# Gathering two expert jobs' tokens with one product, pairing attention units, and a sixth weight buffer

## The chip, the cores and the metric

The kernel runs on one core of a Trainium2 chip. The metric is the device time of one launch in microseconds (us). A core has a matrix engine (TensorE, PE in the rows), which loads a stationary operand ("weight load", PEld) and streams a moving one past it; a vector engine (DVE), a scalar engine (ACT), GpSimd (POOL), a sync engine (SP) that here only issues transfers, and 16 DMA engines. Matrix results land in PSUM, all other on-chip data in SBUF.

## The reference

Two networks run one behind the other on 256 tokens of 1024 features, in fp32.

```python
def first_block(...):                    # depth 2
    for i in range(2):
        u = rmsnorm(h, norm_mix[i])
        h = h + (dsw_mixer if i == 0 else moba_mixer)(u, ...)     # attention a, attention b
        h = h + sq_relu_mlp(rmsnorm(h, norm_ffn[i]), ffn_w1[i], ffn_w2[i])
# dsw_mixer: 3 groups of 8 heads, logits + rel_bias[bucket(dist * dilation)], band masks,
#            the groups' outputs weighted by softmax of their log-sums; moba_mixer: 16 heads

def second_block(x, c, ctx, ...):        # depth 2
    mod = silu(c) @ mod_w[i] + mod_b[i]  # shifts, scales, gates
    yx, yc = (_mixer_ab if i == 0 else _mixer_cd)(...)   # grouped attention, 8 heads, 2 key heads;
                                                         # with a convolution (AB) or a pooling (CD)
    x = x + g1 * yx                      # ctx, 256 tokens, too in layer 0
    out = _moe(tokens, ...)              # 512 tokens in layer 0, 256 in layer 1

def _moe(h, ...):                        # 32 experts, 2 for each token
    xb = h_pad[tok]                      # the tokens of one expert, gathered
    hid = silu(xb @ w_gate[e]) * (xb @ w_up[e])
    return (hid @ w_down[e]) * wt        # added back to the tokens' rows
```

## The kernel before

The stages follow one another, with parts of the next stage pulled into the one that runs (`defer` and `tick` put small steps between matmuls). In the profiled execution they stand about here: 0 to 152 us attention a's projection, to 230 its attention units and output, to 440 the first feed-forward part, to 548 attention b, to 840 the second feed-forward part with the context half of mixer AB, to 1085 the rest of AB and the routing, 1086 to 1616 the experts of layer 0 ("MoE0"), to 1775 mixer CD and the routing, 1778 to 2242 the experts of layer 1 ("MoE1").

**Weights.** All big weights come in units of 1 MB, in the order of one list, issued by SP (`pump`, L242). A unit goes into a ring of RING = 5 SBUF buffers, into smaller rings in some stages, or into SBUF that a stage leaves free; a unit is issued when `consumed` reports that an earlier one has been used.

**Bias table** (`bias_vectors`, L683 to L694). Relative-position biases for 40 heads are made early, in the first projection: four matmuls (one for each of the 3 groups of 8 heads, one for 16 heads) multiply the 33 x heads table `rb` with one-hot rows `oh`. Each result, 8 or 16 partitions of 384 numbers, is copied to `b`, and a POOL-issued DMA writes it 32 times to the DRAM buffer `bd` (the 32 copies let `Bias.fetch` read 128 shifted rows, L709).

**Attention units.** A unit is one head's or some heads' logits for 128 queries (`Attention`, `Unit`). `feed` issues the logits of one unit (L883 for attention a and b, L1155 for the grouped mixers) and its exponentials; `step` transposes a unit's probabilities (L780) and multiplies them with the values (L791). With `pair` 2 (all but attention a) the value products of two units are issued alternately. A head's 64 features lie in partitions 0 to 63 or 64 to 127, so a logits matmul uses half of the rows of TensorE; the heads of one unit all use the same half. Up to three units are fed ahead. PSUM has 6 buffers `acc` and 2 buffers `trp`.

**Modulation.** Between the units, `step` of the modulation multiplies 2 units `fw` of `mod_w` (L631); the next two are issued from there (L615).

**Experts** (L1910 to L2254). Two experts make a job of 128 slots, one expert in each half. 16 jobs; MoE0 has a 17th, "extra". For a job, DVE makes the one-hot matrix `P` (token x slot, `match`, L1924). The tokens are kept as two fp32r parts `hi` and `lo`, token rows on partitions. `gather` multiplies `P` as the stationary operand with the tokens (L1935 `hi`, L1936 `lo`; 128 x 512 each, 16 in MoE0 with four token tiles, 8 in MoE1 with two), giving slots on partitions; ACT copies that to `G`. `turn` transposes `G` in 8 blocks (L1949), and DVE copies to `XT`, features on partitions. `project` (L2000) multiplies `XT` with gate and up weights, `hidden_T` (L2023) transposes the product, `down` (L2038) multiplies with the down weights, `combine` (L2047) adds the result to the tokens. While job i runs, job i+1's gather and its transposes stand between `hidden_T` and `down`, and in the middle of `down`.

Behind job OVER = 7 in MoE1, and behind "extra" (index 8) in MoE0, stands a loop for experts with too many tokens (L2216 to L2232). It is skipped in the run shown, where nothing overflows. Before it the last job is combined; after it the next job is gathered from the start (`first_half`).

## Time and profile before

| | us |
|---|---|
| median of 3 runs | 2248.01 |
| lowest, highest | 2244.2, 2254.72 |
| the profiled execution's own time | 2244.44 |
| its span in the trace | 2242.3 |
| busy in the span: PE / DVE / ACT / POOL | 2055.0 / 1052.6 / 802.8 / 482.9 |

A row of the profile's timeline has the start in us, the length in us, the engine, the line, the operation, the tile written and those read, the shapes, and a count of like instructions in a row; in brackets stands how long the engine was idle before, and what released it. A matmul's end is modelled: neighbours overlap in the rows, and the distance of their starts is what one costs.

### The profile page before, as it was taken

What the parts mean: (1) busy time and instruction counts of PE and PEld (TensorE: products, weight loads), DVE (VectorE), ACT (ScalarE), POOL (GpSimd) and SP (SyncE); (2) the same over time, 40 slices, a digit from 0 to 9 for tenths busy, and PEclk for the clock granted to TensorE, in tenths of its full rate; (3) what the DMA queues carried; (4) which work ended last, traced back from release to release, by engine and by line L of the source; (5) the groups of instructions that cost most, each with busy time, mean ns of one, the idle gap of its engine ahead of it and who ended that gap; (6) DMA issues with size and microseconds to landing.
All of it is one profiled execution on the core that took longest, in us unless ns stands there. A gap on an engine that the chain in (4) does not pass through costs nothing. (4 is left out here: it accounts for less than half of the span.)

```text
span 2242.3 us, 28204 instructions
## 1 busy us (share of the span) xinstructions
PE 2055.0 (92%) x10811; PEld 1296.0 (58%) x10811; DVE 1052.6 (47%) x2077; ACT 802.8 (36%) x1454; POOL 482.9 (22%) x431
## 2 busy tenths in 40 slices
PE   7699999999998699689799997999889799989998
PEld 5476888776997588357444453444365544433443
DVE  6544645664758955966533332333463422222222
ACT  5344544555666566544211111111164411211111
POOL 1000010100116610403233232323330111211111
PEclk9899999999999999688899999999999899999999
DMA  9966677775654343104699996999742699999998
GB/s 259 269 240 239 207 252 264 232 264 176 204 180 151 123 140 112 36 32 162 268 409 406 403 405 269 406 405 402 298 148 80 243 418 421 420 420 384 421 420 346
DMA packets 160701, 612.97 MB, mean 273 GB/s; under 512 B 10599, under 2 KB 16135, under 8 KB 111280
## 3 DMA queue, kind: packets, MB, share of 16 engines
q1 hardware_dynamic: 155744, 596.86, 69.4%
q0 software_dynamic: 4384, 13.51, 3.0%
q8 instruction: 87, 1.43, 0.3%
q10 hardware_dynamic: 432, 0.74, 0.1%
q14 instruction: 54, 0.44, 0.1%
HBM read 607.90 MB, written 3.16 MB: 273 GB/s over the span
## 5 line engine op out<-in xcount | busy, mean ns | idle before, releaser
L2000 PE MATMUL acc<-w,XT 128*64 128x512 f32 x1856 | 430.6, 594 | 2.9 <-DMA w<-in_ex_up_dram 2.8
L301 DVE TENSOR_TENSOR w<-w 128x1024 fp32r<-128x1024 f32 x244 | 306.7, 1270 | 196.7 <-ACT w L300 192.2
L300 ACT ACTIVATE w<-w 128x1024 fp32r<-128x1024 f32 x252 | 264.4, 1057 | 187.8 <-PE acc L321 92.5
L2000 PEld LDWEIGHTS acc<-w,XT 128*64 128x64 f32 x1856 | 140.8, 137 | 252.6 <-issue 230.7
L2059 POOL TENSOR_TENSOR X<-X,tm 128x512 f32<-128x512 f32 x124 | 155.7, 1283 | 426.6 <-DVE tm L2057 426.6
L2057 DVE TENSOR_TENSOR tm<-acc,gate 128x512 f32<-128x512 f32 x196 | 129.7, 687 | 213.0 <-PE acc L2047 167.1
L2038 PE MATMUL acc<-w,hT 128*64 128x512 f32 x912 | 215.3, 598 | 1.5 <-ACT hT L2026 1.5
L363 PE MATMUL acc<-hi,w 128*128 128x256 f32 x576 | 165.6, 288 | 8.0 <-ACT qn L1094 3.8
L364 PE MATMUL acc<-lo,w 128*128 128x256 f32 x576 | 163.1, 283 | 0.8 <-POOL lo L490 0.8
L365 PE MATMUL acc<-hi,w 128*128 128x256 f32 x576 | 162.9, 283 | 0.7 <-DVE w L301 0.7
L321 PE MATMUL acc<-w,lo 128*128 128x512 f32 x368 | 150.3, 408 | 1.7 <-POOL lo L1368 1.6
L319 PE MATMUL acc<-w,hi 128*128 128x512 f32 x336 | 143.5, 427 | 7.7 <-ACT hi L1367 6.3
L320 PE MATMUL acc<-w,hi 128*128 128x512 f32 x336 | 137.6, 410 | 9.0 <-DVE w L301 8.8
L2059 POOL TENSOR_TENSOR C<-C,tm 128x512 f32<-128x512 f32 x64 | 79.6, 1275 | 286.5 <-DVE tm L2057 286.5
L2026 ACT ACTIVATE hT<-trp 128x512 f32<-128x512 f32 (+1 forms) x33 | 19.6, 593 | 325.7 <-PE trp L2023 325.7
L2017 DVE SCALAR_TENSOR_TENSOR hd<-sg,ws,acc 128x512 f32<-128x512 f32 (+1 forms) x33 | 36.2, 1098 | 187.6 <-issue 95.8
L2038 PEld LDWEIGHTS acc<-w,hT 128*64 128x64 f32 x912 | 62.4, 136 | 101.4 <-issue 99.1
L363 PEld LDWEIGHTS acc<-hi,w 128*128 128x128 f32 x576 | 110.5, 192 | 11.2 <-ACT qn L1094 4.0
L1304 POOL TENSOR_TENSOR cy<-cy,tap 128x256 f32<-128x256 f32 x90 | 88.8, 1007 | 119.4 <-ACT tap L1303 68.3
L365 PEld LDWEIGHTS acc<-hi,w 128*128 128x128 f32 x576 | 111.4, 193 | 0.9 <-DVE w L301 0.9
L320 PE MATMUL acc<-w,hh 128*128 128x512 f32 x256 | 102.2, 399 | 10.6 <-DVE w L301 10.4
L417 ACT ACTIVATE Yh<-acc 128x512 fp32r<-128x512 f32 x63 | 37.6, 598 | 206.5 <-PE acc L2038 202.8
(431 smaller groups left out, 3671.8 us busy)
## 6 DMA issues: line engine op xcount, KB each, us to landing
w<-in_ex_gate_dram SPq DMA_DIRECT2D x118, 1024.0 KB, 11.3
w<-in_ex_up_dram SPq DMA_DIRECT2D x118, 1024.0 KB, 12.5
w<-in_ex_down_dram SPq DMA_DIRECT2D x118, 1024.0 KB, 9.5
w<-in_ffn_w_dram SPq DMA_DIRECT2D x64, 1024.0 KB, 5.3
fw<-in_mod_w_dram SPq DMA_DIRECT2D x48, 1024.0 KB, 7.4
w<-in_a_w_qkv_dram SPq DMA_DIRECT2D x17, 1024.0 KB, 13.0
w<-in_w_in_ab_dram SPq DMA_DIRECT2D x14, 1024.0 KB, 5.2
w<-in_b_w_qkv_dram SPq DMA_DIRECT2D x12, 1024.0 KB, 5.3
```

The lines of the kernel that those rows point to most:

```text
L300: nc.scalar.activation(wh, w, AF.Copy)
L301: self.engine.tensor_tensor(wl, w, wh.bitcast(F32), op=OP.subtract)
L319: nc.tensor.matmul(ps[:, :n], xh, wh, start=first, stop=False)
L320: nc.tensor.matmul(ps[:, :n], xh, wl, start=False, stop=False)
L321: nc.tensor.matmul(ps[:, :n], xl, wh, start=False, stop=last)
L363: nc.tensor.matmul(z, wh[:, js], xh, start=k == 0 and j % 2 == 0, stop=False)
L364: nc.tensor.matmul(z, wh[:, js], xl, start=False, stop=False)
L365: nc.tensor.matmul(z, wl[:, js], xh, start=False, stop=k == 7 and j % 2 == 1)
L2000: nc.tensor.matmul(p[self.rows(a)], self.XT[:, 4 * k0 + k, self.rows(a)], units[v + a][:, k], start=k0 + k == 0, stop=4 * k0 + k == 7)
L2038: nc.tensor.matmul(self.p[c][self.rows(a)], self.hT[:, 2 * n + k, self.rows(a)], units[v + a][:, k, s], start=n + k == 0, stop=n + k == 2)
L2057: nc.vector.tensor_tensor(g, p, gates[s][:, c], op=OP.mult)
L2059: add.tensor_tensor(dst, dst, g, op=OP.add)
```

## The change

- `bias_vectors`: the table is widened on DVE so that each head's column stands 32 times (`wide`); ten matmuls of 4 heads each give all 128 partitions at once; DVE and ACT copy the results in turn; 16 DMAs write `bd` from 64 or 128 partitions without repeating a source row. The order of `bd`'s heads changes with it.
- `Attention`: two units are always fed together, their logits matmuls issued alternately, and one unit uses the upper and the other the lower half of the rows. Attention a gets paired value products too. Up to four units are fed ahead.
- Experts: `Group` gathers for two jobs at once: the tokens are the stationary operand (128 x 128 blocks) and `P` of 256 slots moves, so that the result has features on partitions and needs no transposes: 64 matmuls of 128 x 256 for two jobs in MoE0, 32 in MoE1. Every second job has no gather. The copies to `XT` alternate between ACT and DVE. MoE0's 17th job is gathered alone, at 256 columns.
- The loop stands behind job index 8 in both layers, and the job behind it is gathered before it.
- RING is 6; some small tiles are shared by both layers, and a scratch size for POOL's DMA descriptors is given.

```diff
-RING = 5
+RING = 6
...
+            wide = wk.tile([33, 24, 32], F32, name="wide")
+            nc.vector.tensor_copy(wide, b_(rb[:, :, None], [33, 24, 32]))
+
+            for i, h0 in enumerate([*range(0, 24, 4), *range(0, 16, 4)]):
+                g = min(i // 2, 3)
+                p = acc()[:, 0:384]
+                nc.tensor.matmul(p, wide[:, h0:h0 + 4].rearrange("r h c -> r (h c)"), oh[:, g], start=True, stop=True)
+                b = wk.tile([128, 384], F32, name="b", bufs=10)
+                if i % 2:
+                    nc.scalar.activation(b, p, AF.Copy)
+                else:
+                    nc.vector.tensor_copy(b, p)
+
+                for a, r, n in [(2 * a, 3 * (h0 % 8) + 6 * a + 2 * g, 2) for a in range(2)] if g < 3 else [(0, 24 + h0, 4)]:
+                    nc.gpsimd.dma_start(bd[r:r + n].rearrange("h c n -> (h c) n"), b[32 * a:32 * (a + n)])
...
+            pair = 2
+
+            def __init__(self, us):
+                assert len(us) % 2 == 0
+                self.us = us
                 self.a = self.i = self.v = 0
 
-            def prime(self):
-                while self.a < min(3, len(self.us)):
-                    self.feed()
-
             def feed(self):
-                if self.a < min(self.i + 3, len(self.us)) and self.us[self.a].ok():
-                    self.us[self.a].logits()
-                    self.us[self.a].exps()
-                    for o, _ in self.us[self.a].outs:
-                        o.summed()
-                    self.a += 1
+                us = self.us[self.a:self.a + 2]
+                if us and self.a < self.i + 3 and all(u.ok() for u in us):
+                    for _ in zip_longest(*(u.logits() for u in us)):
+                        pass
+                    for u in us:
+                        u.exps()
+                        for o, _ in u.outs:
+                            o.summed()
+                    self.a += 2
                     return True
                 return False
 
             def step(self):
 
-                if self.a < self.i + 3 and self.feed() and self.a < self.i + 3 and self.v == self.i:
+                if self.feed() and self.a < self.i + 3 and self.v == self.i:
...
-                        nc.tensor.matmul(p[:, i], self.QT[r, h // 2, t * 128:(t + 1) * 128], self.KT[r, h // 2, 0:nk],
-                                         start=True, stop=True)
+                        yield nc.tensor.matmul(p[:, i], self.QT[r, h // 2, t * 128:(t + 1) * 128], self.KT[r, h // 2, 0:nk],
+                                               start=True, stop=True)
...
-                att = Attention(us, 1 if G > 1 else 2)
+                att = Attention(us)
...
-                        att.prime()
+                        att.feed()
...
+        PAIRED = (0, 5, 4, 1, 2, 7, 6, 3)
...
-                    for hs in ([0, 2], [1, 3], [4, 6], [5, 7]) if s else [[h] for h in range(8)]:
+                    for hs in ([0, 2], [5, 7], [4, 6], [1, 3]) if s else [[h] for h in PAIRED]:
...
+                class Group:
+                    def __init__(self, sides, pool=wk):
+                        self.sides, self.pool = sides, pool
+                        self.n = 256 if pool is wk else 128 * len(sides)
+                        P = wk.tile([128, NT, 256], F32R, name="P")
+                        self.P = P[:, :, 0:self.n]
+                        self.places = [(s, P[:, :, 128 * i:128 * i + 128]) for i, s in enumerate((sides * 2)[:self.n // 128])]
+                        for s, p in self.places[:len(sides)]:
+                            s.P = p
+                        self.p = {}
+                    def match(self, a=0, b=NT):
+                        for s, p in self.places:
+                            s.match(p, a, b)
+                    def collect(self, j, tiles):
+                        if j not in self.p:
+                            self.p[j] = acc()[:, 0:2 * self.n].rearrange("p (k s) -> p k s", k=2)
+                        for t4 in tiles:
+                            for k in range(2):
+                                for i, h in enumerate(route.tokens(t4, slice((2 * j + k) * 128, (2 * j + k + 1) * 128))):
+                                    nc.tensor.matmul(self.p[j][:, k], h, self.P[:, t4], start=t4 == order[0] and k + i == 0,
+                                                     stop=t4 == order[-1] and k + i == 2)
+                    def gather(self, tiles=order):
+                        XT = self.pool.tile([128, 8, self.n], F32, name="XT")
+                        for i, s in enumerate(self.sides):
+                            s.XT = XT[:, :, 128 * i:128 * i + 128]
+                        for j in range(4):
+                            self.collect(j, tiles)
+                            p = self.p.pop(j)
+                            if NT == 4:
+                                if j % 2:
+                                    nc.vector.tensor_copy(XT[:, 2 * j:2 * j + 2], p)
+                                else:
+                                    nc.scalar.activation(XT[:, 2 * j:2 * j + 2], p, AF.Copy)
...
-                cur, prev = side(0), None
+                prev = None
+                sides = {0: side(jobs[0]), 1: side(jobs[1])}
+                group = Group([sides[0], sides[1]])
 
                 if NT > 2:
-                    cur.match(2, 4)
-                    for h2 in range(2):
-                        cur.collect(h2, order[:2])
+                    group.match(2, 4)
+                    for j in range(4):
+                        group.collect(j, order[:2])
                 route.finish()
-                cur.match(0, 2)
-                for h2 in range(2):
-                    cur.gather(h2, order[-2:])
-                for h2 in range(2):
-                    cur.turn(h2)
+                group.match(0, 2)
+                group.gather(order[-2:])
                 half = NT // 2
                 u = u0
                 for i, j in enumerate(jobs):
-                    loop = jobs[i] == ("extra" if EXTRA[l] else OVER)
-                    nxt = side(jobs[i + 1]) if i + 1 < len(jobs) and not loop else None
-                    if nxt:
-                        nxt.match()
+                    cur = sides.pop(i)
+                    if i % 2:
+                        sides.update((n, side(jobs[n])) for n in range(i + 1, min(i + 3, len(jobs))))
+                        group = Group(list(sides.values())) if sides else None
+                        if group:
+                            group.match()
+                    nxt = sides.get(i + 1)
                     for m in range(2):
                         p = cur.project(m, u)
                         if i == 0 and m == 0:
...
                                 prev.combine(t4)
                     cur.hidden_T()
                     if nxt:
-                        nxt.gather(0)
-                        nxt.gather(1)
+                        if i % 2:
+                            group.gather()
                         nxt.turn_P()
-                        nxt.turn(0)
                     for n in range(2):
                         cur.down(n, u)
                         if nxt and n == 0:
-                            nxt.turn(1)
                             nxt.weights()
                         if i + 1 == len(jobs) and n:
                             for t4 in range(NT):
...
                     if i == 0:
                         during()
                     u += cur.units
-                    prev, cur = cur, nxt
-                    if loop:
+                    prev = cur
+                    if i == OVER + 1:
                         for t4 in order:
                             prev.combine(t4)
+                        prev = None
...
-                        prev, cur = None, side(jobs[i + 1])
-                        cur.first_half()
...
-    nc = _bacc.Bacc("TRN2", target_bir_lowering=False, num_devices=1)
+    nc = _bacc.Bacc("TRN2", target_bir_lowering=False, num_devices=1, dynamic_dma_scratch_size=4096)
```

The removed functions and loops stand in the listing above; the loop's body changes in the same manner.

On PE, in attention a's units, where the trace stands at about 161 to 168 us. `L780` (now `L788`) transposes probabilities `S`, `L883` (`L891`) makes logits, `L791` (`L799`) multiplies with values, `L631` is the modulation. Before:

```order
L780 MATMUL trp_1250<-cst_75,S_1180 128x128 x4
L780 MATMUL trp_1256<-cst_75,S_1180 128x128 x2
L883 MATMUL acc_1262<-KT_195,QT_194 128x256 x2
L883 MATMUL acc_1266<-KT_195,QT_194 128x256
L791 MATMUL acc_1272<-PT_1228,V_196 64x128 x6
L631 MATMUL acc_1279<-fw_1130,cs_116 32x512 x4
```

After:

```order
L788 MATMUL trp_1290<-cst_75,S_1212 128x128 x4
L788 MATMUL trp_1296<-cst_75,S_1212 128x128 x2
L891 MATMUL acc_1302<-KT_197,QT_196 128x256
L891 MATMUL acc_1306<-KT_197,QT_196 128x256
...
L891 MATMUL acc_1311<-KT_197,QT_196 128x256
L891 MATMUL acc_1314<-KT_197,QT_196 128x256
L631 MATMUL acc_1324<-fw_1170,cs_118 32x512 x4
...
L799 MATMUL acc_1347<-PT_1278,V_198 64x128
L799 MATMUL acc_1347<-PT_1289,V_198 64x128
```

Two units' logits, in four `acc` buffers, now stand alternately, and so do two units' value products.

On PE, in MoE0, between one job's `hidden_T` (`L2023`, now `L1989`) and the next job's `project` (`L2000`, now `L1966`); `L1967` (`L1942`) transposes `P`, `L1974` (`L1949`) gathers the slots' weights, `L2038` (`L2004`) is `down`. Before, in each job (the rows left out alternate as the two above them):

```order
L2023 MATMUL trp<-cst,hd 128x128 x4
L1935 MATMUL acc<-hi_9015,P 128x512
L1936 MATMUL acc<-lo_9016,P 128x512
...
L1967 MATMUL trp<-cst,P 128x128 x4
L1949 MATMUL trp<-cst,G 128x128 x4
L2038 MATMUL acc<-w,hT 64x512 x8
L1949 MATMUL trp<-cst,G 128x128 x4
L1974 MATMUL acc<-wt_8844,P 128x4 x4
L2038 MATMUL acc<-w,hT 64x512 x8
L2000 MATMUL acc<-w,XT 64x512 x16
```

After, in the jobs with even index; in those with odd index 64 rows `L2136 MATMUL acc<-P,hi 128x256` and `acc<-P,lo` stand between the first and the second row:

```order
L1989 MATMUL trp<-cst,hd 128x128 x4
L1942 MATMUL trp<-cst,P 128x128 x4
L2004 MATMUL acc<-w,hT 64x512 x8
L1949 MATMUL acc<-wt,P 128x4 x4
L2004 MATMUL acc<-w,hT 64x512 x8
L1966 MATMUL acc<-w,XT 64x512 x16
```

The transposes `L1949` of before are gone, and the gather stands in every second job.

On PE, behind the skipped loop of MoE1 (MoE0 is the same with 16 gather rows). Before:

```order
L2220 UNCONDITIONAL_BRANCH
L1935 MATMUL acc<-hi,P 128x512
...
L1967 MATMUL trp<-cst,P 128x128 x2
L1949 MATMUL trp<-cst,G 128x128 x8
L1974 MATMUL acc<-wt_13862,P 128x4 x2
L2000 MATMUL acc<-C,XT 64x512
```

After:

```order
L2237 UNCONDITIONAL_BRANCH
L1966 MATMUL acc<-w,XT 64x512 x32
L1989 MATMUL trp<-cst,hd 128x128 x4
L2136 MATMUL acc<-P,hi 128x256
```

The next job's `project` now follows the branch at once; the gather that stands behind it is that of the two jobs after it.

## Rows read from the trace of the kernel before

**Rows 1.** Page, section 2: moved bytes in 40 slices of 56.06 us each.

```profile
GB/s 259 269 240 239 207 252 264 232 264 176 204 180 151 123 140 112 36 32 162 268 409 406 403 405 269 406 405 402 298 148 80 243 418 421 420 420 384 421 420 346
```

**Rows 2.** Timeline of PE, the bias matmuls and the first modulation step.

```profile
35.18 2.74 PE L690 MATMUL acc<-oh,rb 33*8 33x384 f32 x8 [0.29 <-DVE rb L685]
88.74 1.94 PE L631 MATMUL acc<-fw,cs 128*32 128x512 f32 x8 [17.24 <-DMA fw<-in_mod_w_dram]
```

**Rows 3.** Transfers, 35 to 90 us: POOL's queue (packets, MB, share); issues to landing.

```profile
q0 software_dynamic: 1280, 3.54, 57.8%
...
bd<-b POOLq DMA_DIRECT2D x3, 384.0 KB, 17.9
```

**Rows 4.** Windows: length, busy of PE, PEld, DVE, ACT, POOL; clock, DMA share, GB/s.

```profile
150.00:216.00 66.00, 64.35 (x436) 45.39 (x434) 30.03 (x88) 29.48 (x58) 4.50 (x8) 1.00 0.74 251
...
1365.00:1370.00 5.00, 5.00 (x16) 3.92 (x15) 0.00 (x0) 0.60 (x1) 0.00 (x0) 0.60 0.00 0
```

**Rows 5.** Timeline of PE, attention a's units.

```profile
152.52 2.23 PE L883 MATMUL acc<-KT,QT 64*128 64x256 f32 x18
...
161.04 0.93 PE L883 MATMUL acc<-KT,QT 64*128 64x128 f32 x6
...
162.71 1.56 PE L883 MATMUL acc<-KT,QT 64*128 64x256 f32 x6
164.19 1.52 PE L791 MATMUL acc<-PT,V 128*64 128x128 f32 x12
```

**Rows 6.** Timeline of DVE: a reduction of logits in attention a.

```profile
163.97 0.69 DVE L887 CUSTOM_DVE_ANT_0 S<-acc,bt 128x512 f32<-128x512 f32 x1 [0.73 <-PE acc L883]
```

**Rows 7.** Timeline of PE: values in attention b, logits in AB and CD.

```profile
511.89 1.09 PE L791 MATMUL acc<-PT,V 128*64 128x128 f32 x16
...
928.24 5.49 PE L1155 MATMUL acc<-KT,QT 64*128 64x512 f32 x6 [5.94 <-ACT QT L1104]
...
1717.09 1.12 PE L1155 MATMUL acc<-KT,w 64*128 64x512 f32 x2
```

**Rows 8.** Timeline of PE, one job of MoE0.

```profile
1210.08 7.04 PE L2000 MATMUL acc<-w,XT 128*64 128x512 f32 x32
...
1229.89 0.39 PE L1935 MATMUL acc<-hi,P 128*128 128x512 f32 x1
1230.12 0.40 PE L1936 MATMUL acc<-lo,P 128*128 128x512 f32 x1
...
1232.65 0.60 PE L1949 MATMUL trp<-cst,G 128*128 128x128 f32 x4
...
1241.18 1.03 PE L2000 MATMUL acc<-w,XT 128*64 128x512 f32 x4
```

**Rows 9.** Timeline of PE and PEld, a feed-forward product of before.

```profile
324.97 0.28 PE L363 MATMUL acc<-hi,w 128*128 128x256 f32 x1
325.09 0.28 PE L364 MATMUL acc<-lo,w 128*128 128x256 f32 x1
...
324.97 0.19 PEld L364 LDWEIGHTS acc<-lo,w 128*128 128x128 f32 x1
```

**Rows 10.** Timeline of PE: MoE0 behind the loop, and its last job.

```profile
1363.51 0.77 PE L1935 MATMUL acc<-hi,P 128*128 128x512 f32 x1 [9.22 <-DVE P L1924]
1364.07 0.63 PE L1936 MATMUL acc<-lo,P 128*128 128x512 f32 x1
1364.50 0.63 PE L1935 MATMUL acc<-hi,P 128*128 128x512 f32 x1
...
1372.08 1.51 PE L2000 MATMUL acc<-w,XT 128*64 128x512 f32 x6
...
1606.50 7.09 PE L2038 MATMUL acc<-w,hT 128*64 128x512 f32 x32 [0.75 <-ACT hT L2026]
```

**Rows 11.** Timeline of PE, the start of MoE1.

```profile
1773.09 0.77 PE L1935 MATMUL acc<-hi,P 128*128 128x512 f32 x1 [0.91 <-DVE P L1924]
...
1778.58 0.65 PE L2000 MATMUL acc<-w,XT 128*64 128x512 f32 x1
```

More of the change, by code (lines that the diff above doesn't have):

```diff
@@ L968, in attention_layer @@
                             rs = [[g * Hg + h for g in range(G)] for h in hs]
-                            part_ = slice(3 * j, 3 * j + 3) if G > 1 else slice(j, 4, 2)
+                            part_ = slice(j, 2 * per * G, 2)
                             us.append(BiasUnit(at, t, rs, QT, KT, V, (bias, part_),
@@ L1150, in logits @@
                 nk, n = 128 * self.nkt, len(self.hs)
[L1151 removed]
+                self.P = self.wk.tile([128, 512], F32, name="P", bufs=4)
                 p = acc()
@@ L1513, in run @@
                         o.extra = with_sink
-                        for h in range(8):
+                        for h in PAIRED:
                             us.append(GqaUnit(at, t4, [h], QT, KT, V, 4, o, band[:, t4], sink, low, [("k", 0), ("k", 2)]))
-                    att = Attention(us, 2)
+                    att = Attention(us)
                     def keys(tiles, j0):
@@ L1616, in __init__ @@
                 self.M = T([32], "M", F32R)
-                self.slot = hold.tile([128, NT, NE], F32, name=f"slot{l}")
-                self.wt = hold.tile([128, NT, NE, 2], F32R, name=f"wt{l}")
-                self.run = hold.tile([128, NE], F32, name=f"run{l}")
-                self.before = hold.tile([128, NE], F32, name=f"before{l}")
-                self.none = hold.tile([128, 1], F32, name=f"none{l}")
+                self.slot = hold.tile([128, 4, NE], F32, name="slot")[:, :NT]
+                self.wt = hold.tile([128, 4, NE, 2], F32R, name="wt")[:, :NT]
+                self.run = hold.tile([128, NE], F32, name="run")
+                self.before = hold.tile([128, NE], F32, name="before")
+                self.none = hold.tile([128, 1], F32, name="none")
                 nc.vector.memset(self.none, 0.0)
-                self.over = hold.tile([128, 1], I32, name=f"over{l}")
+                self.over = hold.tile([128, 1], I32, name="over")
                 self.H, self.h, self.p, self.placed = {}, {}, {}, []
@@ L1982, in rows @@
                         return slice(64 * a, 64 * a + 64)
-                    def first_half(self):
-                        self.match()
-                        for h2 in range(2):
-                            self.gather(h2)
-                        self.turn_P()
-                        for h2 in range(2):
-                            self.turn(h2)
-                        self.weights()
                     def project(self, m, u):
@@ L2143, in used @@
                         pass
+                class Group:
[31 more added lines that the diff above has]
+                                    nc.scalar.activation(XT[:, 2 * j:2 * j + 2], p, AF.Copy)
+                                continue
+                            for kk in range(2):
+                                k = 2 * j + kk
+                                sc, sh = mod4[:, 1, k:k + 1], mod4[:, 0, k:k + 1]
+                                if kk:
+                                    nc.vector.tensor_scalar(XT[:, k], p[:, kk], sc, sh, op0=OP.mult, op1=OP.add)
+                                else:
+                                    nc.scalar.activation(XT[:, k], p[:, kk], AF.Identity, bias=sh, scale=sc)
@@ L2223, in moe @@
                                 s = Late(sl, w1)
-                                s.first_half()
+                                late = Group([s], ok)
+                                late.match()
+                                late.gather()
+                                s.turn_P()
+                                s.weights()
                                 for m in range(2):
```

56 lines of the change are left out of this document (5 added, 51 removed).

## The prediction

> **What bounds the kernel now.** I read the slices of moved bytes first [rows 1]: they part the span into stages with different limits. In the slices 21 to 28 the rate is 403 to 409 GB/s except for one of 269; in the last eight it is 418 to 421, but for one of 384 and the last, 346. Elsewhere it is lower and changes. So the transfers may bind in the experts, and the next question is which of PE and DMA ends last there. In MoE0 the timeline gives it: two jobs start 31.10 us apart (1210.08 and 1241.18), and the rows between carry no idle time [rows 8]. A job takes 12 units of 1 MB (1.049 million bytes); at the 421 GB/s that the later slices reach [rows 1] that is 29.9 us, 1.2 less than PE needs. MoE0 is PE's, with little room below. MoE1 is the DMA's: with half of the token tiles PE needs less, and the rate stays at 420. There only later starts, holes in the rate and the number of units left count.
>
> The first 230 us are PE's with holes. The largest is one wait of 17.24 us for `fw` at 88.74 [rows 2]. What held that load is seen in the transfers of 35 to 90 us: POOL's queue has 57.8% of the time of all 16 engines for 3.54 MB, and three of its bias writes need 17.9 us each from issue to landing, for 384 KB [rows 3]. The writes come from 8 partitions of the copies. Attention a's units, 150 to 216 us, are PE's too, 64.35 of 66 us busy, with DMA at 0.74 and DVE and ACT below half [rows 4].
>
> **Start and bias.** The wait of 17.24 us goes if the writes no longer choke the queue that `fw` and the projection's weights share. PE gets more to do: 8 records of L690 took 2.74 us, 0.34 each [rows 2]; ten matmuls are 20 records, 6.9 us, so +4.1. The widening and the ten copies join DVE and ACT between the normalisation steps; I put +2 for the projection that waits behind them, a choice, since no row shows them there. The 16 DMAs stand on POOL before the bias reads, which are wanted only at 150 us; POOL works 4.5 of 66 us even there [rows 4], so the longer queue of issues has cover. Sum -17.2 + 4.1 + 2 = **-11**, from -17 (copies hidden) to -2 (the stall becomes one for another load).
>
> **Attention a.** The stage has 16 units, 8 of each kind. Logits cost 1.5 us for a unit of 256 keys and 0.86 for one of 128 (1.56 and 0.93 less the overlap with the next row) [rows 5], together 18.9. What does a pair on different halves of the rows cost? The three units fed at 152.52 tell it: their neighbours are on different halves, three units in a row, 18 records in 2.23 us, where one after the other they would need 1.5 + 0.86 + 1.5 = 3.9 [rows 5]. That is 0.57 of the serial price, so about 8 us go. Values: 12 records take 1.45 us alone, 0.121 each [rows 5]; attention b, which pairs them already, needs 1.02 for 16, 0.064 each [rows 7]. Of some 17 us for 16 units 8 go. Together -16, if nothing else comes last. Two things do. First, the modulation's loads: 0.74 of 66 us is 49 us of DMA [rows 4], so the stage can't lose more than 17. Secondly, a pair of 256-key units takes four of the six `acc` buffers, two hold outputs, and the modulation or the next values need a seventh: PE waits for a reduction of 0.69 us [rows 6] on DVE, in 8 pairs 0.7 each, +6. I take **-10**, from -16 to -3.
>
> **Attention b, AB, CD.** In b only the logits change: 16 units, a little under 14 us, 0.57 of it left, -6 in the best case; reductions again take a part: **-4** (-7 to 0). In the grouped mixers a unit's logits cost 1.06 us at full clock (1.12 in its row) [rows 7]; 8 pairs in each save up to 8.5. But AB's units wait for ACT and run at half clock, 6 records in 5.49 us behind 5.94 of waiting for `QT` [rows 7], so PE's saving is partly idle time there: **-5** (-10 to +2). In CD the units stand between matmuls of the projection, and the softmax chain of each is as long as before: **-4** (-8 to +1). The upper ends stand for the wait that two units must both be ready.
>
> **MoE0.** Before: the gather is 16 matmuls 0.23 apart, 3.7 us, and two groups of four transposes, 0.60 us in the row and some 0.45 without its overlap [rows 8]: 4.6 a job, for 15 jobs 69. After: 64 matmuls of 256 columns for two jobs. The feed-forward product does such ones, each with its own weights, 0.12 us apart [rows 9]; half of 0.233 gives 7.5 a group. Eight groups are 60. In the even jobs only the transposes of `P` stand between `hidden_T` and `down`, so PE waits for the copy `hT`: with nothing between it was 0.75 us [rows 10]; I take 0.5, 8 times, 4. So 69 - 64 = -5.
>
> Behind the loop, PE idled 9.22 us, then gathered and turned at first at half clock, and projected at 1372.08 [rows 10]: 17.8 us from the last combine. In the window 1365 to 1370 the clock is 0.60 and the DMA rate 0 [rows 4]. Now the project follows the branch. Of the 9.22 us the branch and the last combine remain, 6 to 8, since the match of `P` is the end of that wait; I take 7, and 2.6 for the half clock, which now hits the project (12 matmuls of 0.43 instead of 0.23 [rows 10]): -8. At the start, the first gather covers two jobs. MoE1's start shows the price, since there too two tiles are left at that point: 5.5 us from the first gather matmul to the project [rows 11]. After: 32 matmuls at half clock, half of 0.43 each, 6.9, and a copy of 1.2: 8.1, so +2.6. Sum -5 - 8 + 3 = **-11**, from -17 to -3. The DMA's 29.9 us a job leaves room for it: the mean job falls by 0.4 to 30.7.
>
> The Trainium skill, "TensorE: Matmul & The Clock Gate", Part 3, "What overlaps and what doesn't", speaks against this gather: a weight load runs beside matmuls in flight only when its row group is another. Every load of the new gather fills all rows, so by that sentence each would be paid on top. The rows disagree: full-height loads stand beside matmuls 0.12 us apart [rows 9].
>
> **MoE1.** PE's saving counts for nothing where DMA ends last. Three terms remain. The rate of 384 instead of 421 in one slice [rows 1] is the hole left by the gather behind the loop, when `project` reports nothing consumed: 37/421 of 56.06 us, -4.9. One more unit is loaded ahead while CD runs: 1.049 MB at 421 GB/s, -2.5. The start is 2.6 later, as above. Sum **-5** (-8 to +1).
>
> The scratch size and the shared tiles show in no row; with POOL idle most of the time I put 0.
>
> **Sum.** -11 - 10 - 4 - 5 - 4 - 11 - 5 = -50 against the profiled execution's 2244.4: 2194. The median of the runs is 3.6 above that execution, so the forecast is **2198**.
>
> **Rivals.** *Less: the pairs give nothing.* Two units' products overlap, but PE waits for DVE's reductions, for ACT's exponentials or for `fw` instead. Then the 23 us of the four attention stages stay: 2221. For it: the two waits named above and the idle time in AB [rows 7]. Against: DVE and ACT are under half busy in attention a [rows 4]. The same time would come if alternate units didn't overlap at all, the change not doing what it says; the 18 records in 2.23 us speak against it [rows 5].
>
> *Less: the bias stall moves.* 36 to 90 us is short of bytes in any case; if the queue stays full with the 16 writes, the gain is 2 and not 11: 2207. For it: the writes' bytes stay the same. Against: 3.54 MB in over half of all engines' time is a price of the form, not of the bytes [rows 3].
>
> *Slower: the new gather pays its weight loads.* Each load lasts 0.19 us [rows 9]. If it stood on the path, a matmul would cost 0.31, 64 of them 12 us more, and 9 groups in MoE0, which is PE's, 110 us: 2308. It decides from 50 / (9 x 64) = 0.09 us on top of 0.12: with a spacing above 0.2 the whole gain is gone. Against it are the rows at 0.12; for it, that there the weights alternate between other tiles.
>
> By the rule of the skill's page named above the time would be that of this last rival.
>
> *More:* all terms at their better ends, about 2165.
>
> **How the numbers follow.** Forecast 0.70, pairs without gain 0.13, the stall moves 0.09, slower 0.04, more 0.04. The bounds of the terms, taken as independent, give some 25 us on each side of 2198; upwards a little more, for the first rival: 2170 to 2226. A difference of 0.5%, 11 us, is about what a measurement of this kernel can tell from none: 2237 and 2259. Only a part of the first rival's case, with the MoE's terms small as well, falls between them: faster 0.91, same 0.05, slower 0.04.
>
> **What would show it.** At 70 to 90 us no wait for `fw` over 2 us, and bias writes landing in a third of the time. In attention a, two units' L891 records in about 1.7 us and the stage 8 to 12 shorter; a wait there released by DVE would bear out the first rival. In MoE0, L2136 at 0.12 us apart and jobs by turns about 34 and 27 us; at 0.3 the last rival has come. Behind MoE0's loop `project` 8 to 10 us after the last combine. In MoE1 no slice below 410 between its start and its end. The forecast is wrong above all if MoE0's jobs don't shorten, or if the stages before it hand their gain back as waits for weights.

## The result, and the profile after

The changed kernel takes 2218.57 us (median of 4 runs, 2216.97 to 2219.68), the kernel before in the same runs 2247.25; the ratio is 0.9867 (95% interval 0.9842 to 0.9892). That is 29 us less, where 50 were forecast. The profiled execution, the slowest of the four, has a span of 2217.9 us, 24.4 less than before.

The page's section 2 of the changed kernel, moved bytes in 40 slices, answers to [rows 1]:

```profile
GB/s 321 271 262 202 237 249 258 208 266 173 176 194 152 126 159 78 56 48 161 236 420 414 411 413 298 416 416 412 279 152 109 236 420 421 421 421 383 421 421 340
```

The first slice has gained (321 for 259), MoE0 runs at 411 to 420, and the slice of 384 in MoE1 is still there, with 383.

Where the 24.4 us came from is read from PE's timelines by the same instructions in both kernels: steps of the modulation (`fw`), which stand in the stages up to 543 us, the transposes of `xn` at 837 us, then `hidden_T`. The table gives how much earlier (-) or later each starts than in the kernel before; the last column is the span. Each line is one execution. Kernels whose start is the same code differ there by 2.7 us (-10.3 to -13.0), and later stages with the same code differ by more: in attention a, where no_loop, old_bias, ring5 and single_groups have the changed kernel's code, the five gain 0.4 to 3.9 us, the changed kernel the least. In attention b the same five lose 9.0 to 9.9.

| kernel | start, 145 | att. a, 258 | before b, 493 | att. b, 544 | AB, 837 | MoE0 first, 1104 | MoE0 last, 1605 | MoE1 first, 1795 | end |
|---|---|---|---|---|---|---|---|---|---|
| changed | -11.2 | -11.6 | -10.1 | -1.1 | +0.1 | -7.5 | -20.2 | -22.7 | -24.4 |
| late_back | -11.1 | -16.6 | -16.7 | -15.7 | -16.3 | -24.6 | -37.3 | -42.2 | -42.8 |
| single_bias | -10.3 | -10.8 | -10.8 | -6.8 | -7.9 | -16.0 | -28.7 | -31.3 | -33.2 |
| no_loop | -11.4 | -13.9 | -12.4 | -2.6 | -2.9 | -10.5 | -37.0 | -39.2 | -45.8 |
| old_bias | +1.0 | -1.2 | -1.2 | +8.5 | +8.6 | +2.4 | -11.4 | -14.3 | -14.4 |
| back_dve | -12.9 | -19.4 | -17.8 | -19.2 | -19.0 | -28.0 | -41.5 | -44.4 | -46.2 |
| ring5 | -13.0 | -16.9 | -15.4 | -5.5 | -6.0 | -13.3 | -26.1 | -28.6 | -27.6 |
| single_groups | -12.8 | -15.5 | -15.5 | -5.7 | -5.5 | -6.3 | +33.3 | +33.1 | +34.6 |
| loop_pool | -11.3 | -16.5 | -16.5 | -18.1 | -17.3 | -26.4 | -39.9 | -45.8 | -51.4 |
| single_back | -12.7 | -10.9 | -9.3 | -9.9 | -9.1 | -23.8 | -36.7 | -42.2 | -44.2 |
| pool_ring5 | -11.1 | -18.1 | -16.5 | -18.2 | -16.7 | -31.4 | -44.1 | -49.6 | -52.7 |

The first line tells the case: the start won 11 us, attention a nothing, and attention b gave 9 back, so that at 837 us all was gone. What is left comes from AB, MoE0 and CD.

**Start.** PE's timeline of the changed kernel has no wait at the modulation's first steps, and the transfers of 35 to 90 us answer to [rows 3]:

```profile
35.73 11.08 PE L692 MATMUL acc<-oh,wide 33*128 33x384 f32 x20 [0.85 <-DVE wide L687]
80.97 1.92 PE L631 MATMUL acc<-fw,cs 128*32 128x512 f32 x16
```

```profile
q0 software_dynamic: 1344, 3.54, 23.6%
...
bd<-b POOLq DMA_DIRECT2D x12, 96.0 KB, 4.1
```

The same 3.54 MB take 23.6% of the engines' time and not 57.8%.

**Attention.** PE's timeline in attention a and b. Two units' logits, 12 records, now take the time of one (1.57 us beside the 1.56 of [rows 5]). But PE waits for `R`, one over the softmax sums, and for `fw`, and stretches at half clock follow (3.14 us for the modulation's 16 records at 185.58, where the granted clock is 0.60, and 1.92 at full clock):

```profile
164.62 1.57 PE L891 MATMUL acc<-KT,QT 64*128 64x256 f32 x12
...
170.57 1.07 PE L631 MATMUL acc<-fw,cs 128*32 128x512 f32 x8 [1.10 <-DMA fw<-in_mod_w_dram]
173.73 1.30 PE L631 MATMUL acc<-fw,cs 128*32 128x512 f32 x8 [2.09 <-DMA fw<-in_mod_w_dram]
...
184.60 1.04 PE L834 MATMUL trp<-cst,R 128*128 128x128 f32 x4 [2.39 <-DVE R L829]
185.58 3.14 PE L631 MATMUL acc<-fw,cs 128*32 128x512 f32 x16
...
498.95 1.14 PE L891 MATMUL acc<-KT,QT 64*128 64x256 f32 x8
500.97 0.44 PE L788 MATMUL trp<-cst,S 128*128 128x128 f32 x2 [0.88 <-ACT PT L790]
501.34 1.20 PE L799 MATMUL acc<-PT,V 128*64 128x128 f32 x16
504.21 0.63 PE L834 MATMUL trp<-cst,R 128*128 128x128 f32 x4 [1.68 <-DVE R L829]
...
511.75 0.63 PE L834 MATMUL trp<-cst,R 128*128 128x128 f32 x4 [2.86 <-DVE R L829]
...
524.33 0.44 PE L788 MATMUL trp<-cst,S 128*128 128x128 f32 x2 [1.74 <-ACT PT L790]
...
529.33 1.09 PE L834 MATMUL trp<-cst,R 128*128 128x128 f32 x4 [2.71 <-DVE R L829]
...
538.53 0.63 PE L834 MATMUL trp<-cst,R 128*128 128x128 f32 x4 [2.87 <-DVE R L829]
```

In attention b alone the four waits for `R` are 10.1 us; in attention a two waits for `R` are 4.2 us and three for `fw` 4.1. `R` needs the exponentials of both units of the last pair. DVE's rows that finish it, in the changed kernel and before:

```profile
503.64 0.43 DVE L829 COPY R<-rd 128x512 f32<-128x512 f32 x1
```

```profile
514.54 0.43 DVE L821 COPY R<-rd 128x512 f32<-128x512 f32 x1
```

PE's rows of before that answer to those from 498.95 on:

```profile
510.83 1.13 PE L883 MATMUL acc<-KT,QT 64*128 64x256 f32 x4
511.89 1.09 PE L791 MATMUL acc<-PT,V 128*64 128x128 f32 x16
512.91 1.92 PE L631 MATMUL acc<-fw,cs 128*32 128x512 f32 x16
514.76 0.44 PE L780 MATMUL trp<-cst,S 128*128 128x128 f32 x2
515.13 0.71 PE L883 MATMUL acc<-KT,QT 64*128 64x128 f32 x4
515.77 0.66 PE L826 MATMUL trp<-cst,R 128*128 128x128 f32 x4
```

From the start of the last logits to the finished `R` it took 4.1 us before (510.83 to 514.97), and PE had 3.9 us of other rows to put behind these logits. For a pair it takes 5.1 us (498.95 to 504.07), and two rows of 1.6 us stand there; the modulation now comes behind `R`.

**MoE0.** The gather's matmuls are 0.12 us apart, each with another block of tokens as weights; behind the loop the project comes 7.9 us after the last combine:

```profile
1245.72 0.28 PE L2136 MATMUL acc<-P,lo 128*128 128x256 f32 x1
1245.84 0.28 PE L2136 MATMUL acc<-P,hi 128*128 128x256 f32 x1
...
1350.78 5.52 PE L1966 MATMUL acc<-w,XT 128*64 128x512 f32 x14 [7.92 <-DVEq L2233]
```

**MoE1.** The hole, in windows of 5 us (length, busy of PE, PEld, DVE, ACT, POOL, clock, DMA share, GB/s):

```profile
2025.00:2030.00 5.00, 5.00 (x26) 1.68 (x24) 0.64 (x3) 0.03 (x1) 0.00 (x0) 1.00 1.01 419
2030.00:2035.00 5.00, 5.00 (x26) 1.69 (x24) 1.38 (x2) 1.20 (x2) 0.00 (x0) 1.00 0.55 228
2035.00:2040.00 5.00, 5.00 (x23) 1.87 (x20) 0.52 (x1) 0.60 (x1) 0.00 (x0) 1.00 0.58 197
```

PE is busy through it. What SP's queue waited for, between 1990 and 2045 us (total, times, longest):

```profile
SPq L2233 <- SPq L2233: 18.8, 8, 2.5
```

The line of before that answers to it, in the same stretch:

```profile
SPq L2216 <- SPq L2216: 18.8, 3, 13.9
```

L2233 and L2216 are the branch around the overflow loop. SP, which issues the weights, stands there for 18.8 us in both kernels. In the changed kernel each of the eight waits ends as a transfer lands. The last transfer issued ahead of the branch lands at 2035.42 us, the last wait ends at 2035.43, and the next transfer is issued at 2036.01, when none is left under way.

### The profile page after: what moved, and what is told of

Same layout as the page of the kernel before. It is cut to its first block, busy times and chain, and to the rows that moved or that the text cites. A ratio compares the mean times of both kernels' runs of the same rounds, so it can differ in the third digit from the quotient of the medians.

```text
span 2217.9 us, 28427 instructions
## 1 busy us (share of the span) xinstructions
PE 2010.5 (91%) x10991; PEld 1273.2 (57%) x10991; DVE 1037.8 (47%) x2033; ACT 773.9 (35%) x1379; POOL 487.4 (22%) x443
## 3 DMA queue, kind: packets, MB, share of 16 engines
HBM read 607.90 MB, written 3.16 MB: 276 GB/s over the span
## 5 line engine op out<-in xcount | busy, mean ns | idle before, releaser
L1966 PE MATMUL acc<-w,XT 128*64 128x512 f32 x1856 | 437.2, 600 | 18.8 <-DVEq L2233 10.7
L1966 PEld LDWEIGHTS acc<-w,XT 128*64 128x64 f32 x1856 | 139.0, 138 | 282.6 <-issue 253.5
L2023 DVE TENSOR_TENSOR tm<-acc,gate 128x512 f32<-128x512 f32 x196 | 129.6, 686 | 217.9 <-PE acc L2013 172.2
L2004 PE MATMUL acc<-w,hT 128*64 128x512 f32 x912 | 215.8, 598 | 6.0 <-ACT hT L1992 6.0
L2004 PEld LDWEIGHTS acc<-w,hT 128*64 128x64 f32 x912 | 62.7, 136 | 110.5 <-issue 99.0
L363 PEld LDWEIGHTS acc<-hi,w 128*128 128x128 f32 x576 | 111.3, 193 | 10.8 <-ACT qn L1102 4.0
L2136 PE MATMUL acc<-P,hi 128*128 128x256 f32 x544 | 104.5, 291 | 8.9 <-issue 6.6
L364 PEld LDWEIGHTS acc<-lo,w 128*128 128x128 f32 x576 | 111.4, 193 | 1.4 <-POOL lo L490 1.1
## 6 DMA issues: line engine op xcount, KB each, us to landing
w<-in_ex_gate_dram SPq DMA_DIRECT2D x118, 1024.0 KB, 13.3
w<-in_ex_up_dram SPq DMA_DIRECT2D x118, 1024.0 KB, 14.3
w<-in_a_w_qkv_dram SPq DMA_DIRECT2D x17, 1024.0 KB, 10.3
```

The costliest lines, as they stand in the source:

```text
L363: nc.tensor.matmul(z, wh[:, js], xh, start=k == 0 and j % 2 == 0, stop=False)
L364: nc.tensor.matmul(z, wh[:, js], xl, start=False, stop=False)
L1966: nc.tensor.matmul(p[self.rows(a)], self.XT[:, 4 * k0 + k, self.rows(a)], units[v + a][:, k], start=k0 + k == 0, stop=4 * k0 + k == 7)
L2004: nc.tensor.matmul(self.p[c][self.rows(a)], self.hT[:, 2 * n + k, self.rows(a)], units[v + a][:, k, s], start=n + k == 0, stop=n + k == 2)
L2023: nc.vector.tensor_tensor(g, p, gates[s][:, c], op=OP.mult)
```

## The experiments

Each edit is to the changed kernel, or to the experiment named.

### late_back: the transposes of R a tick later

```diff
...
-                    defer(1, back)
+                    self.back = back
+                    defer(2, lambda: self.back and self.back())
...
```

> The changed kernel with one edit: the transposes of R (one over the softmax sums) are issued two ticks after R is computed, not one, so that a pair's logits or the modulation stand on PE between the values and them. Theory A (the attention stages gave their gain back because PE stands at R: 10.1 us of such waits in attention b, 4.2 in attention a, and half clock behind them): 9 to 15 us faster than the changed kernel, 2204 to 2210, with no wait for R over 0.5 us in attention b. Theory B (feeding two units lengthens the chain over DVE and ACT, and PE waits for the next thing in it, whatever is moved): 0 to 3 faster, 2216 to 2219, with waits for P or PT in the place of those for R.

Measured: 2201.95 us, ratio 0.9806 (0.9788 to 0.9824), 16.6 us faster than the changed kernel. Attention b loses 1 us and not 9, which no kernel without this edit and with pairs comes near. Attention a ends at -16.6 and not -11.6; the four kernels with the edit gain 5.2 to 7.0 us there, the five without it 0.4 to 3.9. Theory A stands, a little above its range. PE's timeline has no wait for DVE's `R` left in b; two of 2.11 for ACT's copy of it have come:

```profile
502.50 0.65 PE L788 MATMUL trp<-cst,S 128*128 128x128 f32 x4 [2.11 <-ACT R L835]
...
524.14 0.66 PE L788 MATMUL trp<-cst,S 128*128 128x128 f32 x4 [2.11 <-ACT R L835]
```

That copy stands on ACT behind the exponentials of a pair, and PE waits for the `trp` buffer that it holds. The waits for `PT` are as before the edit (0.87 and 1.72 us).

### single_bias: attention a and b one unit at a time

```diff
...
-                att = Attention(us)
+                att = Attention(us, 1 if G > 1 else 2, False)   # feed one unit, up to three ahead
...
```

> The changed kernel with attention a and b fed one unit at a time, as before the change (attention a with single values too); the grouped mixers AB and CD stay paired. Theory A (feeding pairs lost about 9 us in attention b and won about nothing in attention a, while AB and CD won 4 and 3): 6 to 10 faster than the changed kernel, 2209 to 2213. Theory B (the pairs are worth what the prediction said, 14 us in both, and something else took it): 10 to 14 slower, 2229 to 2233.

Measured: 2209.02, ratio 0.9827 (0.981 to 0.9844), 9.5 faster than the changed kernel: theory A by the sum. By the table 5.7 us of it stand at the end of attention b, 5.0 of them won in b; the rest comes in stages with the same code. Single units still lose 4.0 us in b against the kernel before. Their waits there are not longer (3.9 us, 4.2 before), but the granted clock is 0.91 in b's 482 to 538 us, where it was 1.00 in the 493 to 544 us of before; in the changed kernel it is 0.89. So of the 9 us lost in b this run puts 5 down to the pairs as the change made them; that pairs cost 9.5 us in these two stages isn't shown.

### no_loop: without the overflow loop and its flush

```diff
-                    if i == OVER + 1:
-                        for t4 in order:
-                            prev.combine(t4)
...
-                                nc.vector.tensor_scalar(at, at, 1.0, None, op0=OP.add)
```

> The changed kernel without the overflow loop and the flush around it in both expert layers (what is left out is the treatment of experts with too many tokens, which these inputs don't need). Theory A (the hole in MoE1's transfers is SP's own stop at the loop's branch, where it waits 18.8 us until every transfer that it has issued has landed; the gather that was moved has nothing to do with it): the hole goes, 5 us, and in MoE0 10 to 14 us of halt behind the last combine go: 2199 to 2204, with no stretch under 410 GB/s in MoE1. Theory B (the hole comes from late consumption by PE, in whatever order): the hole stays in part, since the ring still runs full: 2205 to 2209.

Measured: 2199.86, ratio 0.9788 (0.9767 to 0.9809), 18.7 faster. From MoE0's first job to its last it gains 26.5 us and the changed kernel 12.7, and from MoE1's first job to the end 6.6 and 1.7: 13.8 and 4.9 more, around the two loops. Both windows around the old place of the loop run full:

```profile
1950.00:2000.00 50.00, 47.30 (x202) 17.98 (x201) 9.33 (x18) 4.46 (x8) 7.49 (x6) 1.00 1.01 420
2000.00:2050.00 50.00, 46.88 (x221) 19.56 (x220) 11.80 (x22) 7.33 (x14) 7.55 (x6) 1.00 1.01 420
```

The two skipped loops with their flushes cost the 18.7 us. Whether SP's stop or PE's late consumption makes the hole this run doesn't tell, since both went; loop_pool does.

### old_bias: the bias table as before

```diff
-            wide = wk.tile([33, 24, 32], F32, name="wide")
...
+            for g in range(4):
...
+                nc.gpsimd.dma_start(rows_, b[0:nh, None, :].to_broadcast([nh, 32, 384]))
...
-                            part_ = slice(j, 2 * per * G, 2)
+                            part_ = slice(3 * j, 3 * j + 3) if G > 1 else slice(j, 4, 2)
```

> The changed kernel with the bias table made as before the change (4 matmuls, copies on 8 or 16 partitions, 4 writes that repeat each row 32 times). Theory A (the start's 11 us come from the bias writes alone and stay to the end): 9 to 12 slower than the changed kernel, 2228 to 2231, with a wait of over 15 us for fw at about 88 us. Theory B (a part of the start's gain was lost again in attention a, which waits for fw when it comes early): 4 to 7 slower, 2223 to 2226, with attention a's units taking less time than in the changed kernel.

Measured: 2229.51, ratio 0.9926 (0.9902 to 0.995), 10.9 slower. The wait is back, and the 10 to 12 us at the start last to the end: theory A.

```profile
88.40 1.94 PE L631 MATMUL acc<-fw,cs 128*32 128x512 f32 x8 [18.74 <-DMA fw<-in_mod_w_dram]
```

### back_dve: the copy of R by DVE

```diff
...
-                        nc.scalar.activation(R, p, AF.Copy)
+                        nc.vector.tensor_copy(R, p)
...
```

> late_back with one more edit: the copy of R's transposes from PSUM is made by DVE and not by ACT. In late_back PE waits four times for ACT's copy of R (2.51, 2.11, 2.11 and about 0.5 us), which stands on ACT behind a pair's exponentials and holds one of the two trp buffers. Theory A (each step of the chain that is taken off ACT gives PE its time back): 4 to 7 faster than late_back's 2202, 2195 to 2198, no wait for R over 0.5 us. Theory B (ACT's exponentials bound the attention stages, so PE only waits for PT instead): 2200 to 2203.

Measured: 2198.49, ratio 0.978 (0.976 to 0.98), 3.5 faster than late_back, between the two theories; the intervals overlap. The waits for the copy shrink (2.11 and 2.11 to 1.15 and 1.58 us) but don't go, and `PT` on ACT is as late as before:

```profile
500.37 0.65 PE L788 MATMUL trp<-cst,S 128*128 128x128 f32 x4 [1.15 <-DVE R L835]
...
511.26 0.44 PE L788 MATMUL trp<-cst,S 128*128 128x128 f32 x2 [1.65 <-ACT PT L790]
...
519.76 0.66 PE L788 MATMUL trp<-cst,S 128*128 128x128 f32 x4 [1.58 <-DVE R L835]
```

### single_back: back_dve with single units in attention a and b

The edits of back_dve and of single_bias together.

> back_dve (R's transposes a tick later, their copy by DVE) with attention a and b fed one unit at a time as before the change. It prices the pairs of these two stages once the wait for R is out of the way. Theory A (the pairs are worth about what back_dve's stages gained over the start, 6 in a and 1 to 4 in b): 6 to 10 slower than back_dve's 2198, 2204 to 2208. Theory B (the pairs are worth nothing, the later R alone was the gain): 2196 to 2200.

Measured: 2198.81, ratio 0.9769 (0.9749 to 0.9789): the same as back_dve, as theory B has it. The table shows more, and it isn't B's reason. At 837 us the pairs are worth 9.9 us (-19.0 beside -9.1), which is A's price; 8.3 of them come from attention a. Of these 9.9 us 4.2 are left at MoE0's first job and 2.2 at MoE1's, lost in stages that have the same code in both kernels. Mixer AB takes most: from the transposes of `xn` at 837 us to the first gather PE has the same 1022 instructions in the same order, in 229.4 us in back_dve and 223.5 in single_back. Up to 953 us of back_dve the distance between the two stays within 0.4 us; in the stretch behind that, here of back_dve and then of single_back, 5.9 us go (length, then busy; the clock is the third number from the end):

```profile
953.20:1003.40 50.20, 36.88 (x181) 28.65 (x177) 23.12 (x50) 22.86 (x42) 7.30 (x5) 0.73 0.20 60
```

```profile
962.70:1007.00 44.30, 30.59 (x181) 23.63 (x177) 23.39 (x50) 22.87 (x42) 7.31 (x5) 0.88 0.20 60
```

The same 181 matmuls are 36.9 us busy at a granted clock of 0.73 and 30.6 at 0.88. What made the clock fall in the one is not shown. Ahead of the first difference PE idles 3.16 us in back_dve and 3.15 in single_back, behind the same instructions; then the granted clock is 0.50 in the one (959 to 962 us) and 1.00 in the other (968.5 to 971.5). Nor is it shown that the feeding in a and b has to do with it: pool_ring5, with pairs, has the short AB too (223.6 us), and the other nine kernels with this code take 229.3 to 232.1. single_back and pool_ring5 were measured together, on another chip than back_dve and loop_pool. So what the pairs are worth at the end of the program stays open.

### ring5 and pool_ring5: five buffers

```diff
...
-RING = 6
+RING = 5
...
```

> The changed kernel with 5 ring buffers in place of 6. Theory A (the sixth buffer is one more unit loaded before MoE1, which the DMA bounds, and nothing else): 2 to 3 slower than the changed kernel, 2220 to 2222, the loss all in MoE1. Theory B (the stages before it use it too): 4 to 10 slower, with losses before 1600 us.

Measured: 2217.35, ratio 0.987 (0.9853 to 0.9886), no difference from the changed kernel. From MoE1's first job to the end it loses 1.0 where the changed kernel gains 1.7: the 2.7 us that a unit was priced at. But it came to MoE1 5.9 earlier, of which 1.8 at the start and 3.5 in attention a. Neither theory says that. What follows from one run is little, so the same was tried without the hole:

> loop_pool with 5 ring buffers in place of 6. With the hole gone, MoE1's transfers run from its start to its end without a gap, so a unit less ahead should show. Theory A (one unit more ahead is 1.049 MB at 421 GB/s): 2 to 3 slower than loop_pool's 2193, 2195 to 2196, all of it in MoE1. Theory B (as for ring5 beside the changed kernel, no difference: what one buffer more brings in MoE1 is lost in the stages before it): 2191 to 2194.

Measured: 2190.26 (5 runs, 2189.56 to 2191.73), ratio 0.9729 (0.9714 to 0.9744), beside loop_pool's 2192.75 and 0.9763 (0.9746 to 0.9779): not slower, rather a little faster. Again MoE1 itself is 2.5 us longer (3.1 gained beside 5.6), and again it is reached earlier, by 3.8 us, with 5.6 won in AB and a part lost again. AB's 5.6 us aren't shown to be the buffer's: ring5 has the long AB (230.8 us) with five buffers, single_back the short one (223.5) with six. So the sixth buffer earns its price where it was priced, and the whole doesn't show it, since the stages ahead of MoE1 differ by more from one kernel to the other. What the buffer does to those stages stays open.

### single_groups: the new gather for one job at a time

```diff
...
-                        self.n = 256 if pool is wk else 128 * len(sides)
+                        self.n = 128 * len(sides)      # one side; P in two buffers; a gather in each job
...
```

> The changed kernel with the new gather made for one job at a time, 128 columns: 64 matmuls of 128 x 128 for each job of MoE0 and not 64 of 128 x 256 for two. Theory A (what a gather matmul costs goes by its columns): 0.06 us apart, 3.7 us a job, the same as now in sum: 2214 to 2222. Theory B (the loading of the tokens as weights, 0.12 us at least, bounds them as soon as the columns are fewer): 0.12 us apart, 3.7 us more a job, in 16 jobs about 60: 2270 to 2285.

Measured: 2278.67 in one run, 60 slower than the changed kernel, 52 of them between MoE0's first and last job: theory B in the price. The rows are 0.11 apart for half the columns:

```profile
1232.77 0.27 PE L2136 MATMUL acc<-P,hi 128*128 128x128 f32 x1
1232.88 0.28 PE L2136 MATMUL acc<-P,lo 128*128 128x128 f32 x1
1232.99 0.27 PE L2136 MATMUL acc<-P,hi 128*128 128x128 f32 x1
```

64 x 0.11 = 7 us a job, where the old gather with its transposes took 4.6. Two jobs at once are what makes this form of gather pay. That it is the weight loads which set the 0.11 us is argued; the run shows that the columns don't.

### loop_pool: the loop's own loads on POOL, on top of back_dve

```diff
...
-            nc.sync.dma_start(v, w)
+            eng.dma_start(v, w)                      # eng = nc.gpsimd for the loop's loads
...
-   e = nc.values_load(ei[0:1, 0:1], engines=(mybir.EngineType.SP,), ...)
+   e = nc.values_load(ei[0:1, 0:1], engines=(mybir.EngineType.Pool,), ...)
```

> back_dve with the overflow loop's own weight loads issued by POOL and not by SP, so that SP has no transfers of its own in the loop. Theory A (SP stops at the skipped loop because its queue's transfers must land before it goes on, and this makes the hole of 5 us in MoE1): no stretch under 410 GB/s in MoE1 from its start to its end, 4 to 6 faster than back_dve. Theory B (SP's branch itself, or the other engines, make it): the same time as back_dve, the hole stays.

Measured: 2192.75, ratio 0.9763 (0.9746 to 0.9779), 5.7 faster than back_dve: theory A. SP no longer waits at the branch, and the slice of 383 is now 420, with the loop and the gather behind it where they were, and the table has 5.6 us gained from MoE1's first job to the end, where back_dve has 1.8. MoE0's halt behind the last combine is as long as in back_dve (34.4 us from the job ahead of it to the next in both, 21.6 in no_loop):

```profile
GB/s 323 275 252 219 249 248 256 211 268 182 214 190 137 122 147 113 33 39 171 274 420 417 414 410 298 415 417 413 277 154 115 243 421 421 421 420 420 421 421 333
```

With five buffers this version, pool_ring5, is the fastest of all, 28 us under the changed kernel and 60 under the one before.

## Why the prediction was right and wrong

The sum was -50 against the profiled execution, and -24.4 came; the sign, the bias table, AB, CD and MoE0's mechanism were right, attention and MoE1 were not. The time, 2218.6, is 20.6 above the forecast and near the first rival's 2221: the four attention stages together gave +0.1 where 23 stood. That is the rival's number, but not its way, since AB and CD gave 8.5 and attention a and b lost 8.6.

- **Start, -11: -11.2.** The wait went, and old_bias shows that it was the writes. That the total agrees is partly luck. The ten matmuls cost more than priced: 20 records in 11.08 us, that is 8.3 more than before and not 4.1. They are 0.32 apart up to 37.8 us, near the price, and 0.64 from there on, where the granted clock is 0.50 (1.2 GHz, the lower of its two levels). On the other side three waits for `fw` went, 18.8 us together, and the prediction counted the one of 17.2. -18.8 + 8.3 leaves 0.7 that I did not trace, and the +2 for the copies is not seen.
- **Attention a, -10: -0.4; attention b, -4: +9.** The prices of the products were right: a pair of units in 1.57 us. The step that failed is "Two things do", the list of what comes last: it named `fw` and the reductions. `fw` did come (0.92, 1.10 and 2.09 us in a), the reductions hardly. In b the wait that decided is the one for `R`, at the end of the chain over DVE and ACT: 10.1 us, with 1.6 us of PE's work to cover it where 3.9 stood before. late_back shows it: one deferred step gives 8 us back in b, and 16.6 in all. In a the waits for `R` and for `fw` were alike (4.2 and 4.1), and the -0.4 is the worst of five kernels with that code (up to -3.9). Of the waits named in the first rival, "PE waits for DVE's reductions, for ACT's exponentials or for `fw`", the second comes nearest, since `R` waits for them; but that rival took nothing gained for the worst, and b lost 9 us, 5 of them by the pairs (single_bias).
- **AB, -5: -5.2** (-5.1 at the gather's first matmul, 1067.51 beside 1072.59, from +0.1). **CD, -4: -3.3** (1749.55 beside 1773.09 of [rows 11]). Both sizes are those of one execution: the kernels with this code gain 3.8 to 12.3 us in AB and 2.9 to 6.2 in CD, so that -5 and -4 were met within this spread. Two stretches between the stages, at the ends of the feed-forward parts, lost 1.5 and 1.2.
- **MoE0, -11: -15.1.** The gathers, -5, measured -5.8: jobs take 34.1 and 26.9 us by turns, where 34 and 27 stood. Behind the loop, -8 measured -6.9. The start was mis-sized: +3 stood for a second half of the gather at half clock, after MoE1's row. It measured -2.4: the 32 matmuls ahead of the routing's end start at a granted clock of 0.50 (1067.5 to 1072 us), PE runs them without a break, and from 1072 us on the clock is up; the second 32 run 0.12 apart.
- **The rival of the weight loads** fell: 0.12 us apart throughout. By the Trainium skill, "TensorE: Matmul & The Clock Gate", Part 3, "What overlaps and what doesn't", they would have been paid, since a load overlaps matmuls only in another row group; the rows of the gather disagree, as those of [rows 9] did.
- **MoE1, -5: -0.9.** The start cost +0.8 (6.3 us from the first gather matmul to the project, beside 5.5) and the unit ahead brought 2.7 by ring5. The hole of 4.9 stayed. The step that failed is "the hole left by the gather behind the loop": it was read off a place in time, not off who waited. SP's own line of waits in the trace of before had it. loop_pool shows the cause: SP, which has transfers in the loop's body, waits at the skipped branch until those it has under way have landed; without them it doesn't wait, and the slice runs at 420.

## What to carry to other kernels

When two units are issued as one, price the chain behind them too: ask which result of the pair the matrix engine next wants, and how much of its own work stands between; here that work fell from 3.9 to 1.6 us while the chain grew from 4.1 to 5.1. For a hole in the transfers, read the issuing engine's own waits before blaming the consumer. And a gain in one stage is only sure at the end of the program, and over several executions: the same AB code differed by 5.9 us between two kernels, and the granted clock with it.

## What the runs showed of the hardware

- An fp32r matmul with its own full 128 x 128 weights costs 0.12 us with 256 columns (the changed kernel) and 0.11 with 128 (single_groups), both at a granted clock of 1.00: half the columns save almost nothing.
- A skipped loop whose body has transfers of an engine stops that engine until its transfers have landed: SP 18.8 us in the changed kernel, in steps of up to 2.5 us, as 1 MB lands every 2.5 us at 421 GB/s. With the body's transfers on POOL (loop_pool) SP doesn't stop.
- The granted clock of the same instructions in the same order was 0.73 in one kernel (back_dve, 50.2 us) and 0.88 in another (single_back, 44.3 us), in a stretch in which PE waits often.
